# Up stage of a hybrid attention block: the last transposes of hT in four runs of four, one per step of the weights' stream

## The chip, the cores and the metric

The kernel runs on one core of one Trainium2 chip. The metric is device time in microseconds; of several runs the median is compared. The core has a matrix engine (TensorE, PE in the profile; its weight loads are PEld), a vector engine (VectorE, DVE), a scalar engine (ScalarE, ACT), GpSimd (POOL) and a sync engine (SyncE, SP) that issues most of the DMAs. Each engine works through its own instructions in order and waits for the others by semaphores.

## The reference

One layer of a decoder with 256 tokens and width 2048, in float32. The parts before the place of the change (attention of three kinds, gates, the output projection) end in a residual x. Then comes the feed-forward part:

```python
h2 = rms_norm(x, g_ffn[l])
u = causal_depthwise_conv(h2 @ w_up[l], conv_w[l], conv_b[l])   # width 2 * 5632
u_gate, u_val = jnp.split(u, 2, axis=-1)
x = x + (jax.nn.silu(u_gate) * u_val) @ w_down[l]
```

`rms_norm` divides each row by the root of its mean square and multiplies by a gain per column. The convolution is over three tokens, per channel.

## The kernel before

**Precision.** Each float32 product is made of parts: a weight piece `raw` is loaded, `hi` is its rounded copy (ScalarE, `piece`, L143), `lo` is `raw - hi` (VectorE, L144). Activations are split likewise. `wp` holds four buffers each of `raw`, `hi` and `lo`, so a cast to `hi` waits until TensorE has read the piece four back, and a load waits until the `lo` of the piece four back is made.

**The output projection** (`blocked`, name "o") adds to the residual `xres` in two halves of 1024 columns. Behind each half, two generators `hidden_T(n)` are queued (L1188), one for each 512 columns, n = 0 to 3.

**hT.** `hidden_T(n)` transposes the columns of `xres` to `hT`, the moving operand of the up stage. `transposed` makes two k tiles (one pair): four 128x128 transposes on TensorE into one PSUM bank (L197), two scaled copies on ScalarE (L183) and two subtractions on VectorE (L186). Pairs are named by their first k tile: n = 0 and 1 make pairs 0 to 6 during the second half of the output projection, n = 2 makes 8 and 10, n = 3 makes 12 and 14; 12 lies in the large tile, 14 in a tile of its own (`hT_rest`). `square_part` then takes the squares' sums of the 512 columns (L622, ScalarE). After n = 3 the root of the mean is made (`row_rstd`: L629, L607 to L612, with two activation table loads on ScalarE), written to DRAM by POOL (`rstd_row`, L1160, 256 single floats) and read back as a row for all partitions (`rbc`, L1161). The norm's row factor is thus applied only after the up product.

**The up stage** (L1274 on) goes through 11 groups of 512 channels, each with a gate half (s = 0) and a value half (s = 1). Each half is 8 steps; a step loads two k tiles of `w_up` (a piece, written u_s_k here: half s, first k tile k; the tile names in the rows below end in a buffer number), and TensorE makes 16 matmuls of it: for two k tiles and four channel tiles a `hi` matmul (L1289, 512 columns) and a `lo` matmul (L1290, 256 columns). After each step `tick()` lets up to two queued generators go one stretch on, to their next `yield`; a generator that yields a number sits out so many ticks. Step k is the one that uses k tiles k and k + 1, so hT's pair k is needed in step k of the first group.

**After the products**, `first_convs` and `second_convs` handle the first group: copies from PSUM (L1225, L1226), then `taken`: multiply by `rbc` (L1235, VectorE), the taps (L1240 to L1242), SiLU, and the split of the product. The first use of `rbc` is in the value half of the first group.

**What sets the order.** Program order by the generators' ticks, refined by a scheduler that places instructions on each engine's list; instructions given to `in_order` or `pin` keep their place. Two loads of the down stage's `kept` sums (T4, tile `raw_t_d` in the rows) share the buffers of the squares' waste output (`junk`), so they wait on SP's list for the squares.

Of the kernel before, what the change touches and what calls it, by code (L numbers as in the profile page):

```python
# [43 lines left out]
def hybrid_block(  # L44
# [38 lines left out]
    def bank(name):  # L83
        return pp.tile([P, 512], F32, tag="bank", name=name)
# [46 lines left out]
    def pin(ins):  # L131

        if pinned[0]:
            tc.keep_in_program_order(ins)
# [45 lines left out]
    def split_scaled(dsts, srcs, gs):  # L180

        for dst, src, g in zip(dsts, srcs, gs):
            pin(nc.scalar.activation(dst[:, :S], src, AF.Copy, scale=g))  # L183
        for dst, src, g in zip(dsts, srcs, gs):
            pin(
                nc.vector.scalar_tensor_tensor(  # L186
                    dst[:, S:], src, g, dst[:, :S].bitcast(F32), ALU.mult, ALU.subtract
                )
            )

    def transposed(dst, src, g, k, name, n=2):

        ps = bank(f"{name}_{k}")
        for j in range(n):
            for t in range(NT):
                pin(
                    nc.tensor.transpose(  # L197
                        ps[:, j * S + t * P : j * S + (t + 1) * P], src[:, t, (k + j) * P : (k + j + 1) * P], ident
                    )
                )  # L200
        js = range(n)
        split_scaled([dst(k + j) for j in js], [ps[:, j * S : (j + 1) * S] for j in js], [g(k + j) for j in js])
# [414 lines left out]
    def square_part(ss, src, n, name, ts=range(NT)):  # L617

        for t in ts:
            sq = junk(f"junk_{name}_{t}_{n}")  # L620
            tc.keep_in_program_order(
                nc.scalar.activation(  # L622
                    sq, src[:, t, n * 512 : (n + 1) * 512], AF.Square, accum_out=ss[:, t, n : n + 1]
                )
            )

    def row_rstd(dst, ss, name):
        tot = sm.tile([P, NT], F32, tag="tot", name=f"tot_{name}")
        nc.vector.tensor_reduce(tot, ss, AX.X, ALU.add)  # L629
        rsqrt_mean(dst, tot, NT, D, name)  # L630
# [517 lines left out]
    rbc = cst.tile([P, S], F32, tag="rbc", name="rbc")  # L1148

    def hidden_T(n):  # L1150
        yield
        transposed(hT, xres, gffn, 4 * n, "hT")
        transposed(hT, xres, gffn, 4 * n + 2, "hT")
        square_part(ssf, xres, n, "f")
        yield
        if n == 3:

            row_rstd(rstd_f, ssf, "f")
            row = dram.tile([NT, P], F32, tag="rstd_row", name="rstd_row")
            nc.gpsimd.dma_start(row.rearrange("t p -> p t"), rstd_f)  # L1160
            nc.gpsimd.dma_start(rbc, row.rearrange("t p -> (t p)").partition_broadcast(P))  # L1161
# [17 lines left out]
    for nb, plan in enumerate(o_plans):  # L1179
        X = blocked(  # L1180
            "o", w_out, nb, nb * PIECE, plan, lambda p, j: mT[p][:, j], lambda p, f: ms[p][:, f], raw_o, t4_o[nb],
            lambda n0, Y: gather(n0, Y, block),
        )
        for n in range(2):
            for t in range(NT):
                o = xres[:, t, nb * PIECE + n * 512 : nb * PIECE + (n + 1) * 512]
                nc.vector.tensor_tensor(o, o, X[t][n], ALU.add)
            later(hidden_T(2 * nb + n))  # L1188
# [211 lines left out]
```

## Time and profile before

| | |
|---|---|
| median of 3 runs | 1460.6 us (1460.43 to 1470.62) |
| profiled execution, its own time | 1459.85 us |
| its span, first to last instruction | 1458.1 us |
| instructions | 20568 |
| bytes moved by DMA | 387.64 MB, mean 266 GB/s |
| up stage on TensorE | from 741.6 us |
| granted TensorE clock | 1.00 |

All times within the execution count from the start of the span. A row of the timeline gives start, duration, engine, line, operation and operands, how many instructions are merged, and in brackets how long the engine sat idle before it and what ended that. Ends of matmuls are modelled, so pace is read from start to start. "DMA to landing" is the time from the issue of a transfer until its last byte is reported. Durations in the prediction are from this one execution.

### The profile page before, as it was taken

Reading aid. Unit: us, or ns where it says so; the run is one execution under the profiler, and the core shown is the slowest. Engines: PE = TensorE matmul, PEld = TensorE weight load, DVE = VectorE, ACT = ScalarE, POOL = GpSimd, SP = SyncE. Lnnn points to the kernel's source line nnn. Section 1 sums busy time; section 2 is a strip of 40 time slices with the busy share of each in tenths; the row PEclk is TensorE's granted clock in tenths of the full one; section 3 lists DMA queues with packets and bytes.
Section 4 is the critical chain, followed back from the end, with each engine's and each line's share of the span. In section 5 each row is a group of like instructions: output and inputs, shape, how many; then the busy total and the mean of one; then the engine's idle time right before and its main releaser. Section 6 shows DMA issues by size and latency. Waiting matters only on the chain.

```text
span 1458.1 us, 20568 instructions
## 1 busy us (share of the span) xinstructions
PE 1452.6 (100%) x7295; PEld 1228.6 (84%) x7295; DVE 1222.1 (84%) x1804; ACT 852.3 (58%) x1210; POOL 21.4 (1%) x52
## 2 busy tenths in 40 slices
PE   9999999999999999999999999999999999999998
PEld 7888888888888888888888888888888888888887
DVE  5788778776898899998987888888888877999878
ACT  6755445464564556546766656556556565676665
POOL 0000010010000000000000000000000000000000
PEclk9999999999999999999999999999999999999999
DMA  8797999777668576788877888888888866789896
GB/s 294 227 351 246 324 330 329 261 256 218 205 210 267 174 227 200 269 269 263 300 214 233 290 273 299 283 269 300 287 278 299 271 197 201 255 282 339 297 333 218
DMA packets 166502, 387.64 MB, mean 266 GB/s; under 512 B 12554, under 2 KB 29854, under 8 KB 162174
## 3 DMA queue, kind: packets, MB, share of 16 engines
q1 hardware_dynamic: 164702, 383.29, 79.7%
q10 hardware_dynamic: 1328, 2.11, 0.4%
q8 instruction: 57, 0.93, 0.3%
q0 software_dynamic: 368, 0.93, 0.2%
q14 instruction: 47, 0.39, 0.1%
HBM read 347.47 MB, written 38.80 MB: 265 GB/s over the span
## 4 chain that ended last, share of the span: by engine, by line
PE 94%; DVE 3%; issue 2%; DMA 1%; POOL 0%; ACT 0%; DVEq 0%; POOLq 0%; ACTq 0%
PE u L1289 22%; PE u L1290 11%; PE xd L362 4%; PE xd L360 4%; PE xd L361 3%; PE xg L362 3%; PE xg L360 3%; PE xg L361 3%; PE s L362 2%; PE f L362 2%; PE s L360 2%; PE f L360 2%; PE f L361 2%; PE b L362 2%; PE s L361 2%; PE b L360 2%
## 5 line engine op out<-in xcount | busy, mean ns | idle before, releaser
L1289 PE MATMUL u<-hT,hi_u 128*128 128x512 f32 x1232 | 428.3, 394 | 0.0
L1290 PE MATMUL u<-hT,lo_u 128*128 128x256 f32 x1232 | 341.3, 277 | 0.0
L144 DVE TENSOR_TENSOR lo_u<-raw_u,hi_u 128x1024 fp32r<-128x1024 f32 x176 | 215.0, 1222 | 73.3 <-ACT hi_u L143 72.5
L1289 PEld LDWEIGHTS u<-hT,hi_u 128*128 128x128 f32 x1232 | 231.0, 188 | 53.6
L143 ACT CAST hi_u<-raw_u 128x1024 fp32r<-128x1024 f32 x176 | 184.7, 1050 | 133.8 <-PE u L1289 99.4
L1290 PEld LDWEIGHTS u<-hT,lo_u 128*128 128x128 f32 x1232 | 231.3, 188 | 0.0
L355 DVE TENSOR_TENSOR lo_d<-raw_d,hi_d 128x1024 fp32r<-128x1024 f32 x88 | 106.8, 1222 | 16.5 <-ACT hi_d L354 14.1
L354 ACT CAST hi_d<-raw_d 128x1024 fp32r<-128x1024 f32 x88 | 91.8, 1054 | 39.3 <-PE xd L361 13.1
L354 ACT CAST hi_g<-raw_g 128x1024 fp32r<-128x1024 f32 (+1 forms) x80 | 77.1, 972 | 49.4 <-PE xg L361 19.4
L355 DVE TENSOR_TENSOR lo_g<-raw_g,hi_g 128x1024 fp32r<-128x1024 f32 (+1 forms) x80 | 88.6, 1119 | 4.1 <-ACT hi_g L354 4.1
L361 PE MATMUL xg<-hi_g,xT 128*128 128x512 f32 x175 | 68.1, 389 | 0.0
L362 PE MATMUL xg<-lo_g,xT 128*128 128x512 f32 x175 | 68.1, 389 | 0.0
L360 PE MATMUL xg<-hi_g,xT 128*128 128x512 f32 x175 | 68.1, 389 | 0.0
L143 ACT CAST hi_f<-raw_f 128x1024 fp32r<-128x1024 f32 (+1 forms) x40 | 38.5, 967 | 46.3 <-PE f L361 29.4
L144 DVE TENSOR_TENSOR lo_s<-raw_s,hi_s 128x1024 fp32r<-128x1024 f32 (+1 forms) x40 | 44.5, 1119 | 23.8 <-ACT hi_s L143 23.8
L1289 PE MATMUL u<-hT_rest,hi_u 128*128 128x512 f32 x176 | 62.0, 394 | 0.0
L143 ACT CAST hi_b<-raw_b 128x1024 fp32r<-128x1024 f32 x32 | 33.7, 1053 | 45.9 <-PE b L361 20.3
L143 ACT CAST hi_s<-raw_s 128x1024 fp32r<-128x1024 f32 (+1 forms) x40 | 38.4, 962 | 37.7 <-PE s L361 26.8
L1240 ACT ACTIVATE y<-u,taps 128x256 f32<-128x256 f32 x88 | 49.6, 596 | 16.8 <-DVE u L1235 16.7
L144 DVE TENSOR_TENSOR lo_f<-raw_f,hi_f 128x1024 fp32r<-128x1024 f32 (+1 forms) x40 | 44.4, 1116 | 17.4 <-ACT hi_f L143 17.2
L362 PE MATMUL xd<-lo_d,aT 128*128 128x512 f32 x148 | 57.6, 389 | 0.0
L360 PE MATMUL xd<-hi_d,aT 128*128 128x512 f32 x148 | 57.6, 389 | 0.0
(551 smaller groups left out, 3482.0 us busy)
## 6 DMA issues: line engine op xcount, KB each, us to landing
raw_u<-in_w_up_dram SPq DMA_DIRECT2D x176, 512.0 KB, 4.8
raw_g<-in_w_in_dram SPq DMA_DIRECT2D x96, 512.0 KB, 4.5
raw_d<-in_w_down_dram SPq DMA_DIRECT2D x63, 512.0 KB, 5.5
pre_d<-in_w_down_dram SPq DMA_DIRECT2D x17, 1024.0 KB, 7.4
kept_d<-pre_d SPq DMA_DIRECT2D x17, 1024.0 KB, 7.0
raw_f<-in_w_in_dram SPq DMA_DIRECT2D x32, 512.0 KB, 5.6
raw_s<-in_w_in_dram SPq DMA_DIRECT2D x32, 512.0 KB, 6.1
raw_t_d<-kept_d SPq DMA_DIRECT2D x25, 512.0 KB, 5.8
```

Of the source, the lines that this page charges most:

```text
L143: pin(nc.scalar.copy(hi[:, :m], raw[:, :m]))
L144: pin(nc.vector.tensor_tensor(lo[:, :m], raw[:, :m], hi[:, :m].bitcast(F32), ALU.subtract))
L354: nc.scalar.copy(hi[:, :n], src)
L355: nc.vector.tensor_tensor(lo[:, :n], src, hi[:, :n].bitcast(F32), ALU.subtract)
L360: fix(nc.tensor.matmul(o, lhsT=ah, rhs=w[0], start=first, stop=False))
L361: fix(nc.tensor.matmul(o, lhsT=al, rhs=w[0], start=False, stop=False))
L362: fix(nc.tensor.matmul(o, lhsT=ah, rhs=w[1], start=False, stop=last))
L1240: nc.scalar.activation(y, u[:, 2:], AF.Identity, scale=tap(2), bias=tap(3))
L1289: nc.tensor.matmul(ps[i], lhsT=hi[:, j, c], rhs=hT(k + j), start=first, stop=False)
L1290: nc.tensor.matmul(ps[i][:, :S], lhsT=lo[:, j, c], rhs=hT(k + j)[:, :S], start=False, stop=last)
```

## The change

`hidden_T` gets two more stops. n = 3 sits out two more ticks before it begins, and n = 2 and n = 3 stop between their two pairs. n = 0 and n = 1 are as before.

```diff
     def hidden_T(n):
-        yield
+        yield 2 if n == 3 else 0
         transposed(hT, xres, gffn, 4 * n, "hT")
+        if n > 1:
+            yield
         transposed(hT, xres, gffn, 4 * n + 2, "hT")
         square_part(ssf, xres, n, "f")
         yield
```

On TensorE the four pairs 8, 10, 12 and 14 stood behind each other after step 2 of the first group (sixteen transposes in a row); now pair 8 stands after step 2, pair 10 after step 4, 12 after step 6 and 14 after step 8. Lines behind the place move down by two (L1235 becomes L1237, L1289 becomes L1291).

ScalarE's list at this place, before; `hi_u` are weight casts, `hT` and `hT_rest` the copies of the pairs, `junk_f_n` the squares of column block n, L608 and L609 the root:

```order
L143 CAST hi_u_0_10_6931<-raw_u_0_10_6930 128x1024
L183 ACTIVATE hT<-hT_6805,gmix_c 128x256 x2
L183 ACTIVATE hT<-hT_6814,gmix_c 128x256 x2
L622 ACTIVATE junk_f_2_6823,ssf<-xres_again 128x512
L622 ACTIVATE junk_f_2_6825,ssf<-xres_again 128x512
L183 ACTIVATE hT<-hT_6827,gmix_c 128x256 x2
L183 ACTIVATE hT_rest<-hT_6836,gmix_c 128x256 x2
L622 ACTIVATE junk_f_3_6846,ssf<-xres_again 128x512
L622 ACTIVATE junk_f_3_6848,ssf<-xres_again 128x512
L143 CAST hi_u_0_12_6953<-raw_u_0_12_6952 128x1024
L608 ACT_TABLE_LOAD
```

And of the change, from the cast of u_0_14 on (ahead of it stand the cast of u_0_12 and the copies of pair 10 with the squares of block 2):

```order
L143 CAST hi_u_0_14_6975<-raw_u_0_14_6974 128x1024
L183 ACTIVATE hT<-hT_6871,gmix_c 128x256 x2
L143 CAST hi_u_1_0_7001<-raw_u_1_0_7000 128x1024
L183 ACTIVATE hT_rest<-hT_6902,gmix_c 128x256 x2
L622 ACTIVATE junk_f_3_6912,ssf<-xres_again 128x512
L622 ACTIVATE junk_f_3_6914,ssf<-xres_again 128x512
L143 CAST hi_u_1_2_7033<-raw_u_1_2_7032 128x1024
L608 ACT_TABLE_LOAD
L608 ACTIVATE nwt_f<-nwa_f 128x2
L609 ACT_TABLE_LOAD
L609 ACTIVATE nwy_f<-nwt_f 128x2
L143 CAST hi_u_1_4_7061<-raw_u_1_4_7060 128x1024
```

The squares of block 3 and the root stood around the cast of u_0_12; now they stand around that of u_1_2, three casts later, and no cast lies between the two table loads.

VectorE's list where the root ends, before, with the sum of the squares (L629) and the factor that POOL writes out (L612):

```order
L629 TENSOR_REDUCE tot_f<-ssf 128x2
L1219 MEMSET u_7022 128x2
L1219 MEMSET u_7024 128x2
L607 TENSOR_SCALAR nwa_f<-tot_f 128x2
L144 TENSOR_TENSOR lo_u_0_12_6954<-raw_u_0_12_6952,hi_u_0_12_6953 128x1024
L144 TENSOR_TENSOR lo_u_0_14_6976<-raw_u_0_14_6974,hi_u_0_14_6975 128x1024
L610 TENSOR_TENSOR nwt_f<-nwy_f 128x2
L611 SCALAR_TENSOR_TENSOR nwt_f<-nwt_f,nwa_f 128x2
L612 SCALAR_TENSOR_TENSOR scales<-nwt_f,nwy_f 128x2
```

And of the change:

```order
L144 TENSOR_TENSOR lo_u_1_0_7002<-raw_u_1_0_7000,hi_u_1_0_7001 128x1024
L186 SCALAR_TENSOR_TENSOR hT_rest<-hT_6902,gmix_c,hT_rest 128x256 x2
L629 TENSOR_REDUCE tot_f<-ssf 128x2
L607 TENSOR_SCALAR nwa_f<-tot_f 128x2
L144 TENSOR_TENSOR lo_u_1_2_7034<-raw_u_1_2_7032,hi_u_1_2_7033 128x1024
L610 TENSOR_TENSOR nwt_f<-nwy_f 128x2
L611 SCALAR_TENSOR_TENSOR nwt_f<-nwt_f,nwa_f 128x2
L612 SCALAR_TENSOR_TENSOR scales<-nwt_f,nwy_f 128x2
```

The factor is made behind the lo part of u_1_2 instead of u_0_14, two pieces later. The first reader of rbc (L1237) stands where it stood, between the lo parts of u_1_12 and u_1_14.

SP's list, before; `raw_t_d` are the two loads that share the squares' buffers:

```order
L142 DMA raw_u_1_2_7032<-in_w_up_dram 128x2x512
L453 DMA raw_t_d_0_11976<-kept_d_0_2252 128x512
L453 DMA raw_t_d_1_12067<-kept_d_1_2414 128x512
L142 DMA raw_u_1_4_7060<-in_w_up_dram 128x2x512
L142 DMA raw_u_1_6_7082<-in_w_up_dram 128x2x512
L142 DMA raw_u_1_8_7104<-in_w_up_dram 128x2x512
```

And of the change:

```order
L142 DMA raw_u_1_4_7060<-in_w_up_dram 128x2x512
L142 DMA raw_u_1_6_7082<-in_w_up_dram 128x2x512
L142 DMA raw_u_1_8_7104<-in_w_up_dram 128x2x512
L453 DMA raw_t_d_0_11976<-kept_d_0_2252 128x512
L453 DMA raw_t_d_1_12067<-kept_d_1_2414 128x512
L142 DMA raw_u_1_10_7126<-in_w_up_dram 128x2x512
```

The two loads moved past three loads of weights.

## The prediction

> **What bounds the kernel now.** I read the page's totals first, then the chain that ended last, then the up stage by windows.
>
> ```profile
> PE 1452.6 (100%) x7295; PEld 1228.6 (84%) x7295; DVE 1222.1 (84%) x1804; ACT 852.3 (58%) x1210; POOL 21.4 (1%) x52
> PE 94%; DVE 3%; issue 2%; DMA 1%; POOL 0%; ACT 0%; DVEq 0%; POOLq 0%; ACTq 0%
> 741.60:763.80 22.20, 22.20 (x135) 19.59 (x134) 17.24 (x30) 16.21 (x28) 0.74 (x1) 1.00 0.79 199
> 786.00:808.00 22.00, 22.00 (x129) 19.25 (x128) 22.00 (x41) 14.57 (x25) 0.00 (x0) 1.00 0.82 273
> ```
>
> The columns of the last two rows are stretch, length, then busy time of PE, PEld, DVE, ACT and POOL, granted clock, DMA share and GB/s. TensorE is busy for the whole of both stretches at a granted clock of 1.00, so nothing it waits for can be shortened here. It can gain only by doing less, and it loses as soon as an operand is late. From 786 to 808 us VectorE has not a moment free either (22.00 of 22.00), and this matters below.
>
> So the question has two halves: what do the four runs cost on TensorE itself, and does any operand come late because other engines' work moved with them?
>
> **The transposes themselves.** Here are TensorE's rows around the one run of sixteen, and a run of four elsewhere that the kernel makes already (between two matmuls of the merge).
>
> ```profile
> 747.12 0.28 PE L1290 MATMUL u<-hT,lo_u 128*128 128x256 f32 x1
> 747.24 1.91 PE L197 MATMUL hT<-ident,xres_again 128*128 128x128 f32 x16
> 748.91 0.47 PE L1289 MATMUL u<-hT,hi_u 128*128 128x512 f32 x1
> 749.22 0.27 PE L1290 MATMUL u<-hT,lo_u 128*128 128x256 f32 x1
> ...
> 473.25 0.39 PE L362 MATMUL b<-lo_b,oT 128*128 128x512 f32 x1
> 473.48 0.60 PE L1040 MATMUL mt<-ident,g 128*128 128x128 f32 x4
> 473.84 0.48 PE L360 MATMUL b<-hi_b,oT 128*128 128x512 f32 x1
> 474.15 0.40 PE L361 MATMUL b<-hi_b,oT 128*128 128x512 f32 x1
> ```
>
> From start to start, sixteen take 748.91 - 747.24 = 1.67 us, and the matmul behind them holds its place for 0.31 us (749.22 - 748.91) instead of 0.23 (473.48 - 473.25): 1.75 us in all. Four take 473.84 - 473.48 = 0.36 us, and the matmul behind them again 0.31 instead of 0.23: 0.44 us. Four such runs are 1.76 us. The change on TensorE is **+0.01 us**. I bound it by nothing gained (0) and by one further such switch of 0.08 us per added run (+0.24).
>
> Does TensorE still get hT in time? A step (two k tiles) lasts 785.04 to 787.82, that is 2.78 us (rows below). Each of the four pairs now has two whole steps between its run and its own use (14 is transposed after step 8 and used in step 14), at least 5.6 us. In that time it waits for one weight cast on ScalarE (1.05 us) and one lo part on VectorE (1.2), and is copied out at 0.7 us per pair on each (751.65 to 752.36), some 3 us together. Hidden, with over 2 us to spare; if that cover were gone, TensorE would stall by what is missing.
>
> **What moves behind them.** The squares of column block 3 (L622) are issued only after pair 14, so they now come after step 8 instead of after step 2, and the whole chain to rbc hangs on them: sum, reciprocal root, two small transfers by POOL.
>
> ```profile
> 747.32 1.05 ACT L143 CAST hi_u<-raw_u 128x1024 fp32r<-128x1024 f32 x1 [1.78 <-PE u L1289]
> 751.65 0.86 ACT L183 ACTIVATE hT_rest<-hT,gmix_c 128x256 fp32r<-128x256 f32 x2
> 752.36 0.67 ACT L622 ACTIVATE junk_f<-xres_again 128x512 f32<-128x512 f32 x1
> 753.59 1.09 ACT L143 CAST hi_u<-raw_u 128x1024 fp32r<-128x1024 f32 x1
> 754.70 1.28 ACT L608 ACT_TABLE_LOAD   x1
> 756.10 1.03 ACT L143 CAST hi_u<-raw_u 128x1024 fp32r<-128x1024 f32 x1
> 757.15 1.28 ACT L609 ACT_TABLE_LOAD   x1
> 758.45 0.20 ACT L609 ACTIVATE nwy_f<-nwt_f 128x2 f32<-128x2 f32 x1
> 759.07 0.16 DVE L612 SCALAR_TENSOR_TENSOR scales<-nwt_f,nwy_f 128x2 f32<-128x2 f32 x1
> 759.53 0.74 POOL L1160 DMA_DIRECT2D rstd_row<-scales  x1 [422.74 <-DVE scales L612]
> 768.56 0.55 POOL L1161 DMA_DIRECT2D rbc<-rstd_row  x1 [8.29 <-DMA rstd_row<-scales]
> ```
>
> Step by step, in the times of this execution. A weight cast waits until TensorE has read the piece four back, and starts 0.08 us after that step's end (747.32 against 747.24). Step 8 now ends at 747.24 + 3 x (0.44 + 2.78) = 756.9; step 10 at 760.1. The cast of u_1_0 runs 757.0 to 758.0, the two copies of pair 14 to 758.7, the two squares (753.59 - 752.36 = 1.23) to 759.9. The cast of u_1_2 must wait for step 10: 760.2 to 761.2. From a cast's end to the end of the exponential it takes 758.65 - 754.68 = 3.97 us with one other cast (1.05) between the two table loads; that cast is no longer there, so 2.92: 764.1. POOL starts 759.53 - 758.65 = 0.88 later, **at 765.0 instead of 759.53**, 5.5 us late.
>
> ```profile
> DMA to landing us min/median/max: 7.6/7.6/7.6
> ...
> 777.49 1.23 DVE L144 TENSOR_TENSOR lo_u<-raw_u,hi_u 128x1024 fp32r<-128x1024 f32 x1 [1.57 <-ACT hi_u L143]
> 778.63 0.42 DVE L1235 TENSOR_TENSOR u<-y,rbc 128x256 f32<-128x256 f32 x1
> 780.66 1.23 DVE L144 TENSOR_TENSOR lo_u<-raw_u,hi_u 128x1024 fp32r<-128x1024 f32 x1
> 783.83 1.23 DVE L144 TENSOR_TENSOR lo_u<-raw_u,hi_u 128x1024 fp32r<-128x1024 f32 x1
> 805.79 1.22 DVE L144 TENSOR_TENSOR lo_u<-raw_u,hi_u 128x1024 fp32r<-128x1024 f32 x1
> ...
> 785.04 0.39 PE L1289 MATMUL u<-hT_rest,hi_u 128*128 128x512 f32 x1
> 787.82 0.39 PE L1289 MATMUL u<-hT,hi_u 128*128 128x512 f32 x1
> 788.05 0.27 PE L1290 MATMUL u<-hT,lo_u 128*128 128x256 f32 x1
> ```
>
> The first row is the landing of rbc. Before the change rbc is there at 768.56 + 7.6 = 776.2, and its first reader, L1235, starts at 778.63, right behind the weight piece ahead of it: 2.4 us of cover. From POOL's start to the landing it takes 16.6 us, so after the change rbc is there at 765.0 + 16.6 = 781.6, and L1235 starts 3.0 us late. It stands in VectorE's order ahead of the lo parts of the weights; these are late with it. The tightest is the one that began at 783.83: done at 785.06, read by TensorE at 788.05, 2.99 us ahead. Next come 805.79 (done 807.01, needed eight steps after 788.05, at 810.2: 3.2) and 780.66 (done 781.89, needed 0.23 after 785.04: 3.4), the former because VectorE has nothing free from 786 to 808 with which to catch up. A delay of 3.0 us uses up 2.99. The stall on TensorE is **0.0 to 0.1 us**.
>
> The price of that cover gone: each further us by which rbc lands later is about a us on TensorE, once, since TensorE's own stall then restores the distance for all later pieces. The landing is the uncertain term. The nearest other rows are the two pairs of the same kind at 182 us.
>
> ```profile
> L897 POOL DMA_DIRECT2D ck_row<-logits x2: 731/796/860, 182.7 to 183.6; - x2
> DMA to landing us min/median/max: 3.0/6.1/9.0
> L899 POOL DMA_DIRECT2D ck<-ck_row x2: 554/562/569, 186.0 to 189.1; - x2
> DMA to landing us min/median/max: 6.9/7.9/9.0
> ```
>
> With 0.3 us between write and read, the shortest pair would be 3.0 + 0.3 + 6.9 = 10.2 us (rbc at 775.2, no wait at all), and the longest 9.0 + 0.3 + 9.0 = 18.3 us (783.3, 1.8 us of stall). I take 16.6, the same two transfers.
>
> The trace speaks for the long one: while the small write is under way the weights crawl.
>
> ```profile
> 762.00:770.00 8.00, 8.00 (x47) 6.98 (x47) 4.31 (x7) 3.34 (x6) 0.55 (x1) 1.00 0.70 45
> 772.35 1.05 ACT L143 CAST hi_u<-raw_u 128x1024 fp32r<-128x1024 f32 x1 [5.28 <-DMA raw_u<-in_w_up_dram]
> ```
>
> From 762 to 770 us all queues moved 45 GB/s against 273 in the window at 786, and a cast waited 5.28 us for its piece. That slump moves along, to about 767.5 to 775.5. It then catches u_1_12 and later pieces; u_1_12 would land at 777.8 as its forerunner did 2.35 us after the slump, its lo part would be done at 780.1, and TensorE wants it two steps before 788.05, at 782.5: hidden, with 2.4 us over. The two loads of d's T4 on SP's queue move behind u_1_8, since they wait for the same squares; they are read only in the down stage, some 450 us on, and cost nothing.
>
> **The sum.** 0.01 for the runs and 0.05 for the stall on a profiled execution of 1459.85 us (span 1458.1), which lies 0.75 below the median of 1460.6. On the median's scale: 1460.7 us. One per cent, 14.6 us, is about what a measurement of this kernel can tell from no change.
>
> **The rivals.** *The cover holds.* If the small write is quicker where it now lies, as the shortest pair at 182 us was, rbc lands before 778.6 and L1235 doesn't wait. Time 1460.6. Against it stands the slump; I give 0.27. The Trainium skill ("DMA: Bandwidth & Descriptors", section on the anatomy of one DMA on the gpsimd path) puts such a transfer at about 2.0 us plus its bytes over 436 GB/s; by it the pair of 1 KB and 128 KB would take some 4.6 us, an estimate, and this rival would be certain. The trace disagrees: 9.0 us until the write is done, 16.6 for both.
>
> *Slower: the landing is later than 781.6.* The place is L1235 on VectorE at the second half of the first group; it decides from 781.6 on, at a us per us, up to 1.8 us by the longest pair; a slump longer by the same amount could take another us from the pieces at 777 to 783. Times of 1461.5 to 1463.5, still within 1%. For it: other loads queue up around the write than before. 0.20. To reach 14.6 us this mechanism would need rbc at 796, for which no row speaks: 0.02.
>
> *It gives time back, or doesn't act.* The order on the engines shows four separate runs, so it acts. A gain on TensorE needs idle time there, and the up stage has none: 0.01 for over 1% faster.
>
> **Chances and range.** The forecast (stall 0 to 1 us, 1460.4 to 1461.6) has 0.50, the covered case 0.27, the later landing 0.20, the rest 0.03. The range runs from 1459.6, the covered case less 1.0 (the profiled execution lay 0.75 below the median without any change), to 1463.3, the long bound with 0.9 us of further slump. Within 1%: 0.97.
>
> **What would show it.** Four runs of four L197 on PE, each 0.36 us; POOL's L1160 near 765 us; L1237 (L1235 before) on VectorE starting near 781.7 with a wait on the DMA of rbc; TensorE's stretch from 741 to 808 with under 1 us idle. I am wrong if TensorE waits for an hT pair, if rbc lands after 785, or if a lo part is late somewhere past 810 us.

## The result, and the profile after

The change costs time. Its median over 22 runs is **1469.26 us** (1460.53 to 1471.42), beside 1460.49 us (1459.59 to 1470.62) for the kernel before, also over 22 runs. The ratio on record is 1.0039, with a 95% interval of 1.0024 to 1.0053 (the quotient of the two medians is 1.0060): within 1%, as forecast, but above the forecast's range (1459.6 to 1463.3).

The median can't be understood without one fact: the executions of this program have two lengths with little in between, at a granted clock of 1.00 in both. Of the change, 15 of 22 took 1469.0 to 1471.4 us and 7 took 1460.5 to 1462.2; of before, 2 of 22 took 1469 or more, and 20 took 1459.6 to 1462.9. I call them long and short executions. The change turns a rare long execution into the usual one.

The first profile of the change caught a short execution (1460.73 us). The change was therefore profiled again, as the first experiment below, and that profile is of a long one (1470.26 us). First the page's totals of the short one:

```profile
PE 1452.4 (100%) x7295; PEld 1228.7 (84%) x7295; DVE 1222.3 (84%) x1804; ACT 851.4 (58%) x1210; POOL 21.4 (1%) x52
```

The same row of the long one:

```profile
PE 1461.6 (100%) x7295; PEld 1233.1 (84%) x7295; DVE 1223.2 (83%) x1804; ACT 852.3 (58%) x1210; POOL 21.4 (1%) x52
```

TensorE makes the same 7295 instructions and is busy all the time in both, 9.2 us longer in the long one. So little of the loss is waiting. The groups of the up stage's matmuls show where it went (columns: count, then busy time and mean ns of one, then idle time before). Before:

```profile
L1289 PE MATMUL u<-hT,hi_u 128*128 128x512 f32 x1232 | 428.3, 394 | 0.0
L1290 PE MATMUL u<-hT,lo_u 128*128 128x256 f32 x1232 | 341.3, 277 | 0.0
```

The long execution of the change:

```profile
L1291 PE MATMUL u<-hT,hi_u 128*128 128x512 f32 x1232 | 436.8, 399 | 0.0
L1292 PE MATMUL u<-hT,lo_u 128*128 128x256 f32 x1232 | 346.1, 281 | 0.1
```

The same matmuls are a little longer each. Since ends of matmuls are modelled, I read the pace from counts: the view of windows, over 300 us in the middle of the up stage, over 90 us behind the last run of transposes. Before:

```profile
850.00:1150.00 300.00, 300.00 (x1733) 262.35 (x1732) 256.43 (x418) 177.36 (x274) 0.00 (x0) 1.00 0.86 286
```

The short execution of the change:

```profile
850.00:1150.00 300.00, 300.00 (x1733) 262.43 (x1732) 256.46 (x420) 177.34 (x273) 0.00 (x0) 1.00 0.86 287
```

The long execution of the change, in which the second row is the stretch of the forecast's stall:

```profile
850.00:1150.00 300.00, 300.00 (x1700) 260.30 (x1699) 251.52 (x406) 172.72 (x263) 0.00 (x0) 1.00 0.83 279
786.00:808.00 22.00, 21.52 (x120) 18.28 (x120) 21.24 (x39) 17.44 (x29) 0.00 (x0) 1.00 0.75 238
```

In 300 us TensorE makes 1733 matmuls in one kind of execution and 1700 in the other, busy throughout (300.00) at a clock of 1.00. From start to start, where the cut ends of the window don't count, a pair of one hi and one lo matmul takes 0.3467 us in before and in the short execution, and 0.3533 in the long one. Single matmuls follow each other at two fixed patterns: the quick one repeats after two pairs (231, 113, 232, 118 ns), the slow one after three (233, 117, 241, 120, 236, 113 ns). I call them the quick and the slow **rhythm**.

The sum of it: of the stage's 1408 pairs, some 25 are slow in before (ahead of its run) or quick in the long execution (between two of its runs); for the other 1383, 6.7 ns each make 9.2 us. TensorE's waits at 786 to 790 us, shown below, cost 1.0 us more. That is 10.2, and from its first matmul to its last the up stage takes 489.84 us before and 500.05 in the long execution: 10.2 more, of the 10.4 us between the two profiled executions (1459.85 and 1470.26).

Where does the rhythm change? Before enters the up stage slow. The run of sixteen at 747.24 (its rows stand in the prediction) leaves it quick: the matmul behind the run is followed by its lo after 0.31 us, and that by the next hi after 0.11. It stays so to the end of the stage. Here are two of the four runs of the change, the third and the fourth, by TensorE's timeline of the short execution:

```profile
753.96 0.60 PE L197 MATMUL hT<-ident,xres_again 128*128 128x128 f32 x4
754.32 0.47 PE L1291 MATMUL u<-hT,hi_u 128*128 128x512 f32 x1
754.63 0.27 PE L1292 MATMUL u<-hT,lo_u 128*128 128x256 f32 x1
754.74 0.40 PE L1291 MATMUL u<-hT,hi_u 128*128 128x512 f32 x1
...
757.17 0.60 PE L197 MATMUL hT<-ident,xres_again 128*128 128x128 f32 x4
757.53 0.48 PE L1291 MATMUL u<-hT,hi_u 128*128 128x512 f32 x1
757.85 0.28 PE L1292 MATMUL u<-hT,lo_u 128*128 128x256 f32 x1
757.96 0.40 PE L1291 MATMUL u<-hT,hi_u 128*128 128x512 f32 x1
```

The difference is in hundredths: 0.31 and 0.11 behind the third run (313 and 113 ns), 0.32 and 0.11 behind the fourth (318 and 117). The third leaves TensorE quick, as before's run of sixteen did. The first, second and fourth leave it slow, in both executions alike. So behind the last run both stream slowly; what made one of them short came later.

It came at the place of the forecast's stall. POOL's and VectorE's timeline, short execution:

```profile
765.49 0.74 POOL L1162 DMA_DIRECT2D rstd_row<-scales  x1 [427.70 <-DVE scales L612]
775.17 0.55 POOL L1163 DMA_DIRECT2D rbc<-rstd_row  x1 [8.95 <-DMA rstd_row<-scales]
...
782.28 0.43 DVE L1237 TENSOR_TENSOR u<-y,rbc 128x256 f32<-128x256 f32 x1 [0.30 <-DMA rbc<-rstd_row]
787.48 1.23 DVE L144 TENSOR_TENSOR lo_u<-raw_u,hi_u 128x1024 fp32r<-128x1024 f32 x1
```

Long execution, with TensorE's rows:

```profile
775.65 0.55 POOL L1163 DMA_DIRECT2D rbc<-rstd_row  x1 [9.50 <-DMA rstd_row<-scales]
783.27 0.42 DVE L1237 TENSOR_TENSOR u<-y,rbc 128x256 f32<-128x256 f32 x1 [0.94 <-DMA rbc<-rstd_row]
...
785.80 0.40 PE L1291 MATMUL u<-hT_rest,hi_u 128*128 128x512 f32 x1
786.59 0.39 PE L1292 MATMUL u<-hT_rest,lo_u 128*128 128x256 f32 x1 [0.39 <-DVE lo_u L144]
786.81 0.39 PE L1291 MATMUL u<-hT_rest,hi_u 128*128 128x512 f32 x1
...
789.28 0.40 PE L1291 MATMUL u<-hT,hi_u 128*128 128x512 f32 x1
789.76 0.39 PE L1292 MATMUL u<-hT,lo_u 128*128 128x256 f32 x1
789.98 0.39 PE L1291 MATMUL u<-hT,hi_u 128*128 128x512 f32 x1
```

rbc was read 0.99 us later in the long one, and there TensorE waited for lo parts, twice: the lo at 786.59 came 0.79 us behind its hi (785.80) instead of 0.23, the one at 789.76 came 0.48 behind instead of 0.24, and the next matmul took 0.1 more to follow each time (786.81 and 789.98). In all 1.0 us. In the short one nothing waited, but it was close. Here are TensorE's weight loads at the piece whose lo part was finished at 788.71 (787.48 + 1.23):

```profile
788.24 0.19 PEld L1291 LDWEIGHTS u<-hT_rest,hi_u 128*128 128x128 f32 x1
788.36 0.19 PEld L1292 LDWEIGHTS u<-hT_rest,lo_u 128*128 128x128 f32 x1
788.60 0.19 PEld L1291 LDWEIGHTS u<-hT,hi_u 128*128 128x128 f32 x1
788.76 0.19 PEld L1292 LDWEIGHTS u<-hT,lo_u 128*128 128x128 f32 x1
```

A lo's weights are otherwise loaded 0.12 us behind the hi's; this time 0.16: it began 0.05 us behind the end of the lo part, as the two loads that waited in the long execution did (786.59 behind 786.53, 789.76 behind 789.71). The matmul itself wasn't late. From 758 to 788 us the pairs took 0.3533 us; from this place on they took 0.3467, and so the execution was short. That this load made the difference is not shown, only that the pace changes there. In the long one the two real waits left the stream slow, 0.3533 to the end of the stage.

### The profile page after: what moved, and what is told of

It is laid out like the page before. It is cut to its first block, busy times and chain, and to the rows that moved or that the text cites. A ratio compares the mean times of both kernels' runs of the same rounds, so it can differ in the third digit from the quotient of the medians.

```text
span 1459.0 us, 20569 instructions
## 1 busy us (share of the span) xinstructions
PE 1452.4 (100%) x7295; PEld 1228.7 (84%) x7295; DVE 1222.3 (84%) x1804; ACT 851.4 (58%) x1210; POOL 21.4 (1%) x52
## 4 chain that ended last, share of the span: by engine, by line
PE 97%; DMA 1%; issue 1%; DVE 0%; SPq 0%; POOL 0%; ACT 0%; POOLq 0%; DVEq 0%
PE u L1291 22%; PE u L1292 11%; PE xg L361 4%; PE xg L360 4%; PE xg L362 4%; PE xd L361 4%; PE xd L362 3%; PE xd L360 3%; PE s L362 2%; PE f L362 2%; PE f L360 2%; PE s L360 2%; PE f L361 2%; PE b L360 2%; PE s L361 2%; PE b L362 2%
## 5 line engine op out<-in xcount | busy, mean ns | idle before, releaser
L1291 PE MATMUL u<-hT,hi_u 128*128 128x512 f32 x1232 | 429.3, 394 | 0.0
L1291 PEld LDWEIGHTS u<-hT,hi_u 128*128 128x128 f32 x1232 | 231.1, 188 | 53.6
L1291 PE MATMUL u<-hT_rest,hi_u 128*128 128x512 f32 x176 | 62.1, 394 | 0.0
```

The lines of the kernel that those rows point to most:

```text
L1291: nc.tensor.matmul(ps[i], lhsT=hi[:, j, c], rhs=hT(k + j), start=first, stop=False)
```

## The experiments

The expectations name their theories by letters. A: the long executions come from rbc's delay, through the lo parts. B: the separate runs disturb TensorE itself, through a slower pace behind them. C: a weight transfer is held up by POOL's small write at its new place. D, which makes B precise: there are two rhythms, and what interrupts the stream decides which one follows. E, formed later as D's rival: each further run of four costs time by itself. All times are medians with their range; each ratio is against runs of the kernel before on the same chip (1460.68, 1459.90 and 1460.08 us in three sets).

### The change again, and its parts one by one

The change, word for word:

> The changed kernel once more, to see an execution of the longer kind (most of its executions took 1469 to 1471 us, some 1461 to 1462, and the profile at hand is one of the short ones). Theory A (rbc comes late, the lo parts behind its first reader on VectorE come late, TensorE waits): two executions in three near 1469.5; in a profile of such a one TensorE has lost some 8 to 9 us, and the loss begins at a matmul that waits for a lo part between 777 and 812 us. Rival B (the four separate runs of transposes disturb TensorE itself): the loss lies between 747 and 758 us, or in a slower pace of matmuls behind it, with no late lo part. Rival C (a transfer is held up by the small write at its new place): the loss begins where a cast waits for a raw piece longer than 6 us.

1470.01 us (1460.02 to 1471.45, 10 runs: 7 long, 3 short), ratio 1.0048 (1.0028 to 1.0067). Its profile is the long one shown above.

**Four runs, but the root as early as before.** Squares of block 2 and 3 and the root keep their places in the steps; pairs 12 and 14 are transposed behind them.

```diff
-        transposed(hT, xres, gffn, 4 * n, "hT")
-        transposed(hT, xres, gffn, 4 * n + 2, "hT")
+        if n < 3:
+            transposed(hT, xres, gffn, 4 * n, "hT")
+            if n < 2:
+                transposed(hT, xres, gffn, 4 * n + 2, "hT")
         square_part(ssf, xres, n, "f")
         yield
+        if n == 2:
+            transposed(hT, xres, gffn, 4 * n + 2, "hT")
...
+            yield
+            transposed(hT, xres, gffn, 4 * n, "hT")
+            yield
+            transposed(hT, xres, gffn, 4 * n + 2, "hT")
```

> Four runs of four as in the change, but the squares of block 3 and the root stay where they were before the change (squares behind step 2, root behind step 4); pair 12 and 14 follow behind steps 6 and 8. Theory A: rbc is read no later than before the change, all executions as before it, 1460 to 1462 us, hardly any at 1469. Rival B: like the change, most executions at 1469 to 1471. Rival C: like before, as the small write lies where it lay.

1470.11 us (1469.71 to 1471.29, 4 runs, all long), ratio 1.0062 (1.0047 to 1.0077). POOL's timeline, a weight load and the window of this kernel (L1298 is lo here):

```profile
758.73 0.74 POOL L1164 DMA_DIRECT2D rstd_row<-scales  x1 [420.68 <-DVE scales L612]
...
775.16 0.19 PEld L1298 LDWEIGHTS u<-hT,lo_u 128*128 128x128 f32 x1 [0.28 <-DVE lo_u L144]
...
850.00:1150.00 300.00, 300.00 (x1700) 260.21 (x1700) 251.61 (x404) 172.37 (x262) 0.00 (x0) 1.00 0.84 279
```

The write starts 0.8 us earlier than before the change, rbc's first reader doesn't wait for it, and the stream is slow all the same. One lo part is late in this profile: its cast had waited 6.25 us for a weight piece, a sign like the one that C names, and the matmul at 775.16 came 0.35 us behind its hi instead of 0.24. That cost 0.22 us with the matmul behind it. The pairs take 0.3533 us from the last run on, ahead of this wait and behind it, so it didn't make the stream slow. A falls in so far as it needs a late rbc; that no wait at all is needed is shown by the next kernel.

**The change without POOL's transfers.** VectorE fills rbc; the norm's row factor is left out.

```diff
-            nc.gpsimd.dma_start(row.rearrange("t p -> p t"), rstd_f)
-            nc.gpsimd.dma_start(rbc, row.rearrange("t p -> (t p)").partition_broadcast(P))
+            nc.vector.tensor_copy(rbc[:, 0:NT], rstd_f)
+            nc.vector.memset(rbc[:, NT:], 1.0)
```

> The change without POOL's two transfers: rbc is filled by VectorE with ones (two columns with the factors), so the output lacks the row factor of the last norm. Nothing waits for rbc any more, and there is no small write to DRAM in the up stage. Theory A and rival C: all executions at 1459 to 1462 us. Rival B: most executions still at 1469 to 1471 us.

1469.82 us (1468.44 to 1470.74, 4 runs, all long), ratio 1.0058 (1.0043 to 1.0073). The window of this kernel:

```profile
850.00:1150.00 300.00, 300.00 (x1700) 260.02 (x1700) 251.60 (x404) 172.39 (x262) 0.00 (x0) 1.00 0.84 279
```

No matmul of the up stage waits, neither transfer is there, and yet TensorE makes 1700 matmuls in the same 300 us. Neither the transfers nor a late lo part are needed for a long execution: A and C both fall as what the long executions need, and the slow pace of B is left.

**One run of sixteen as before, but the root late.** The sum of squares takes in nothing (0 times a column) of the cast of u_1_0, so it waits for that.

```diff
+    newest = [None]
...
-        yield
+        yield 6 if n == 3 else 0
         if n == 3:
+            seen = newest[0][:, 0, 0:1].bitcast(F32)
+            nc.vector.scalar_tensor_tensor(ssf[:, 0, 0:1], seen, 0.0, ssf[:, 0, 0:1], ALU.mult, ALU.add)
...
+                newest[0] = hi
```

> One run of sixteen as before the change, but the root is made to wait for the cast of u_1_0 (zero times a column of it is added to a sum), so that POOL's write starts near 767 us instead of 759.5. Theory A: the longer kind of execution in most runs though the transposes are as before, 1469 to 1471 us. Rival B: as before the change, 1460 to 1462 us. Rival C: like the change, 1469 to 1471.

1466.21 us (1459.91 to 1471.24, 10 runs: 5 long, 5 short), ratio 1.0024 (1.0000 to 1.0049). The profile is of a long one. TensorE's timeline, in which L1293 is hi and L1294 lo:

```profile
785.64 0.39 PE L1293 MATMUL u<-hT_rest,hi_u 128*128 128x512 f32 x1
786.37 0.39 PE L1294 MATMUL u<-hT_rest,lo_u 128*128 128x256 f32 x1 [0.33 <-DVE lo_u L144]
...
789.05 0.40 PE L1293 MATMUL u<-hT,hi_u 128*128 128x512 f32 x1
789.54 0.39 PE L1294 MATMUL u<-hT,lo_u 128*128 128x256 f32 x1
```

From the run of sixteen up to here the stream was quick (0.3467); after the two waits it is slow (0.3533). So a wait can turn it this way too: the waits cost about 1 us, and the 1279 pairs behind them 8.5 (the stage takes 499.36 us, 9.5 more than before's). The late rbc is neither needed for the loss nor harmless: with the transposes of before, five of ten executions are long here, against 4 of 70 of the kernel before.

### Length and place of the runs

**Two runs of eight**, behind steps 2 and 6: the change without its stop between the pairs, and `yield 2 if n == 3 else 0` kept.

```diff
     def hidden_T(n):
-        yield
+        yield 2 if n == 3 else 0
```

> The sixteen transposes in two runs of eight, behind steps 2 and 6. Theory D (the matmul stream of the up stage has two stable rhythms, 0.346 and 0.353 us per hi/lo pair; every run of transposes draws anew which one follows, and it then lasts for the stage unless TensorE is made to wait): whichever rhythm follows the second run at 757 us lasts, so the time is 1460 to 1462 us with pairs at 0.346, or 1469 to 1471 us with pairs at 0.353, and the last run alone decides. Rival E (the more separate runs, the longer; the loss adds up per run): between the two, near 1463 us.

1460.14 us (1459.63 to 1461.77, 9 runs, all short), ratio 1.0003 (0.9993 to 1.0013). E had put it near 1463 us. Both runs leave the stream quick. The second, by the timeline:

```profile
753.21 1.04 PE L197 MATMUL hT<-ident,xres_again 128*128 128x128 f32 x8
754.00 0.47 PE L1289 MATMUL u<-hT,hi_u 128*128 128x512 f32 x1
754.32 0.27 PE L1290 MATMUL u<-hT,lo_u 128*128 128x256 f32 x1
754.43 0.40 PE L1289 MATMUL u<-hT,hi_u 128*128 128x512 f32 x1
```

**The one run of sixteen, a step later** (behind step 4):

```diff
     def hidden_T(n):
-        yield
+        yield 1 if n > 1 else 0
```

> One run of sixteen as before the change, but one step later (behind step 4). Theory D with the run of sixteen leaving the quick rhythm: 1460 to 1462 us, pairs at 0.346 us from the run on. If the place of the run rather than its length sets what follows: 1469 to 1471 us possible. Rival E: 1460 to 1462.

1469.54 us (1468.72 to 1470.12, 3 runs, all long), ratio 1.0065 (1.0045 to 1.0085).

```profile
750.42 1.91 PE L197 MATMUL hT<-ident,xres_again 128*128 128x128 f32 x16
752.09 0.48 PE L1289 MATMUL u<-hT,hi_u 128*128 128x512 f32 x1
752.40 0.28 PE L1290 MATMUL u<-hT,lo_u 128*128 128x256 f32 x1
752.52 0.40 PE L1289 MATMUL u<-hT,hi_u 128*128 128x512 f32 x1
```

The stream leaves this run slow, and no matmul waits. (The root moves a little too in these two kernels: POOL's write starts at 761.91 and 762.70 instead of 759.53. No lo part is late in either profile.) This is the strongest pair of the study: two runs instead of one cost nothing, and the same one run a step later costs all of it. So it isn't the number of runs, nor their length alone. The run of sixteen entered the slow pattern at one place of its three pairs before (the gaps ahead of it 241, 120, 236, 120 ns) and at another here (232, 118, 241, 121).

**The change with sixteen more transposes** behind step 10 (of a weight piece, into a bank that nobody reads), to set the rhythm back:

```diff
+                if (f0, s, k) == (0, 0, 10):
+                    extra = bank("extra")
+                    seen = hi[:, 1, 384:512].bitcast(F32)
+                    for i in range(16):
+                        nc.tensor.transpose(extra[:, (i % 4) * P : (i % 4 + 1) * P], seen, ident)
```

> The change with sixteen transposes more in one run behind step 10 (of a weight piece, into a bank that nobody reads; 1.75 us of work). Theory D: the stream falls into the quick rhythm at 762 us and stays there, 1462 to 1464 us in most executions, 7 us less than the change though it does more. Rival E: 1471 to 1473 us.

1470.35 us (1462.08 to 1472.29, 7 runs: 4 long, 3 short), ratio 1.0052 (1.0029 to 1.0076). I had expected the run to leave the stream quick. In the profiled execution it left it slow (315 and 117 ns). A long run is no reliable cure.

**The kernel before with four more transposes**, in the fifth group, behind step 8 of its gate half: the same lines, with `(f0, s, k) == (16, 0, 8)` and `range(4)`.

> The kernel before the change with four transposes more in the middle of the up stage (group 5 of 11, gate half, behind step 8, near 937 us; 0.44 us of work). Theory D: what follows may be either rhythm; if a run of four leaves the slow one as the last run of the change did, pairs go from 0.346 to 0.353 us there and the time is 1460.5 + 0.4 + about 850 pairs x 0.0071 = 1467 us. If the quick rhythm survives: 1461 us. Rival E: 1461 us.

1466.76 us (1465.28 to 1467.41, 4 runs), ratio 1.0045 (1.0029 to 1.0061). By the timeline, then the window:

```profile
936.06 0.60 PE L1298 MATMUL extra<-ident,hi_u 128*128 128x128 f32 x4
936.41 0.48 PE L1289 MATMUL u<-hT,hi_u 128*128 128x512 f32 x1
936.73 0.28 PE L1290 MATMUL u<-hT,lo_u 128*128 128x256 f32 x1
936.84 0.40 PE L1289 MATMUL u<-hT,hi_u 128*128 128x512 f32 x1
...
850.00:1150.00 300.00, 300.00 (x1711) 261.40 (x1710) 252.54 (x408) 174.44 (x266) 0.00 (x0) 1.00 0.82 281
```

This is the disputed cost by itself. Four transposes, 0.44 us with the switch, far from hT, the root and rbc, make the stage 6.15 us longer than before's (495.99 against 489.84). Pairs take 0.3467 us ahead of them and 0.3533 behind, up to the stage's end at 1238.8: (1238.8 - 936.4) / 0.3533 = 856 pairs, times 6.7 ns, are 5.7 us, and with the run 6.15. The sum closes for the stage. (The profiled execution is 7.34 us longer than before's; its up stage also began 1.25 us later, at 742.84.)

### Is it the alternation, and does each run cost?

**Hi and lo in groups of four.** For each k tile, four hi matmuls and then four lo ones, with the transposes of before and with those of the change.

```diff
+                    cs = [slice(i * P, (i + 1) * P) for i in range(4)]
                     for i in range(4):
-                        c = slice(i * P, (i + 1) * P)
-                        nc.tensor.matmul(ps[i], lhsT=hi[:, j, c], rhs=hT(k + j), start=first, stop=False)
-                        nc.tensor.matmul(
...
+                        in_order(nc.tensor.matmul(ps[i], lhsT=hi[:, j, cs[i]], rhs=hT(k + j), start=first, stop=False))
+                    for i in range(4):
+                        in_order(nc.tensor.matmul(
...
```

> The kernel before the change with the up stage's matmuls in another order: per k tile the four hi matmuls, then the four lo matmuls, instead of hi and lo in turn. If the two rhythms belong to the alternation of 512 and 256 columns (theory D), they are gone: one pace, the same in every execution. From the trace, matmuls of 512 columns follow each other at 0.227 us in the output projection and 128-column transposes at 0.109, so a pair would take 0.336 us, 0.010 less than now, and the time is 1460.5 - 1408 x 0.010 = 1446 us (estimate). If lo matmuls behind each other take as long as now: 1460 us.

> The change with the same other order of the matmuls. Theory D: the same time as the kernel grouped so without the change, within 1 us, as the four runs cost 0.01 us more and there is no second rhythm to fall into (1446 us, estimate). If the runs of four do harm by themselves: 9 us more than that.

1466.81 us (1466.13 to 1467.19) and 1466.99 us (1466.34 to 1467.54), 4 runs each; ratios 1.0044 (1.0026 to 1.0062) and 1.0047 (1.0031 to 1.0062). The window of the first:

```profile
850.00:1150.00 300.00, 300.00 (x1712) 262.16 (x1711) 251.99 (x408) 172.19 (x266) 0.00 (x0) 1.00 0.81 283
```

Both kernels have 1712 matmuls in this window: one pace, 0.3508 us per pair from start to start, between the two rhythms. The hoped-for 1446 us was wrong, since a lo behind a lo still takes 0.118 us and a hi behind a hi 0.233. But with this order the change costs 0.2 us, less than either range is wide. Its price of 9 us belongs to the alternating stream.

**A fifth run of four** in the change without transfers, so that nothing waits: the lines of the sixteen, with `range(4)`.

> The change without POOL's two transfers (rbc filled by VectorE, so the output lacks the row factor of the last norm) and with a fifth run of four transposes behind step 10 (of a weight piece, into a bank that nobody reads; 0.44 us). Without the fifth run all four executions were of the long kind, 1468 to 1471 us. Theory D: the fifth run draws anew: either quick pairs (0.346 us) from 761 us on and 1461 us, or slow ones (0.353) and 1470 us, and since no wait on rbc follows, all executions alike. Rival E (loss per run): 1471 to 1473 us.

1460.95 us (1460.08 to 1470.22, 9 runs: 6 short, 3 long), ratio 1.0019 (0.9993 to 1.0044). The profile is of a short one:

```profile
761.01 0.60 PE L1300 MATMUL extra<-ident,hi_u 128*128 128x128 f32 x4
761.36 0.47 PE L1291 MATMUL u<-hT,hi_u 128*128 128x512 f32 x1
761.68 0.27 PE L1292 MATMUL u<-hT,lo_u 128*128 128x256 f32 x1
761.79 0.40 PE L1291 MATMUL u<-hT,hi_u 128*128 128x512 f32 x1
```

E falls: with one run of four more, six of nine executions are short, against none of four without it, and the median is 8.9 us lower (1460.95 against 1469.82). I had expected all executions to be alike. They aren't. No matmul waits in the profile of a short one, and a long one wasn't profiled; that the same instructions can come out of a run either way is the likely reading, not a shown one.

## Why the prediction was wrong

**The step that failed** is the first term: "The change on TensorE is +0.01 us", bounded by 0 and +0.24. The 0.01 itself is right: each run of four takes 0.36 us and the matmul behind it 0.31 to 0.32, as in the rows used for it. What was wrong is that a run's cost ends with the matmul behind it. The choice of rhythm acts on every pair until something interrupts the stream again, here 1383 pairs at 6.7 ns. The last run of the change leaves the stream slow where before's only run had left it quick: 9.2 us, in about two executions of three. The bound priced one further switch per run; no bound and no rival priced the stream behind it.

The profile of before held the warning. Ahead of the run of sixteen twelve pairs take 4.24 us (742.65 to 746.89), 0.3533 each, and behind it a pair takes 0.3467; I read single gaps around the run and took the pace for a constant.

**The stall through rbc: right in mechanism and place, mis-sized in the landing.** Forecast: POOL's write at 765.0, rbc's reader at 781.7, 0.0 to 0.1 us of stall. Found, in the short and in the long execution: the write at 765.49 and 765.41, the reader at 782.28 and 783.27, and a stall of none in the one execution and 1.0 us in the other. The write took longer than the 8.29 us taken over from before (a wait of 8.95 and 9.50), so the case "later landing" is the one that came. Its arithmetic held: the reader is 3.65 and 4.64 us later than before's 778.63, TensorE itself some 0.8 later (its slow rhythm, and a stage that began 0.1 to 0.2 later), so of the lead of 2.99 some 0.1 should be left in the one and 0.9 be missing in the other. Counted as a stall it is a tenth of the loss. (The longest pair, with rbc at 783.3, gives 1.7 us by the prediction's own sum, not 1.8.) But its second effect, that it can turn the rhythm, wasn't foreseen: of the kernels whose last run left the profiled stream slow, those with the root as late as in the change have 13 short executions in 39 (the change in two sets, and with sixteen more transposes), those with the root earlier or without the transfers have none in 11 (root early, run a step later, no transfers). This fits the weight load at 788.76, but I have only one profile of a short one, and the runs are few.

**"The cover holds"** (0.27) is out: L1237 waited in both profiles. The Trainium skill ("DMA: Bandwidth & Descriptors", section on the anatomy of one DMA) gives a formula by which a 1 KB transfer takes about 2.0 us, an estimate; the waits of 8.95 and 9.50 us behind the write again disagree with it.

**hT in time, T4, the moved slump**: right. No matmul waited for hT. The slump moved: from 767.5 to 775.5 us of the short execution the queues carried 31 GB/s, TensorE was busy for 8.00 of the 8.00 us, and no matmul came late through it.

**Slower by over 1%** was 0.02 and didn't happen: even the long executions are 0.6% above before. The prediction took 1% for about the least that can be told from no change; the intervals here tell 0.4% from none.

**What stays open.** The runs show that a run of transposes, or a wait, can change the rhythm, and how much that costs. The long and short executions that weren't profiled are put to the rhythms by their times alone. The runs don't show what inside TensorE makes two rhythms, nor a rule by which one could tell the outcome of an entry. One regularity of the profiles is no more than that: wherever a run of four was entered from a quick stream (the fourth run of the change, the run in the fifth group), it was left slow. Its place among the runs doesn't decide what a run leaves: the third run left the stream quick in both profiles of the change and slow (314 ns) with the root early. Nor do they show why 4 of 70 executions of the kernel before were long.

## What to carry to other kernels

Where one engine is busy all the time, measure the pace of its stream (instructions per 100 us, or start to start) ahead of and behind each interruption before pricing an insertion by its own duration; two paces in one trace at one clock are a warning that a small edit may choose between them. A repeated profile and some ten runs belong to such a kernel, since one execution may show either pace. In this kernel two runs of eight were free and four runs of four were not; the run of sixteen moved by a step shows that such an outcome doesn't carry over to another place unmeasured.

## What the runs showed of the hardware

- An alternating stream of hi (512 columns) and lo (256) matmuls has two lasting rhythms at a granted clock of 1.00: 0.3467 and 0.3533 us per pair, 1.9% apart, each kept up for over 400 us. Four hi and four lo in turn have one pace, 0.3508.
- In one profile a weight load that came 0.04 us late, without a visible delay of its matmul, was followed by the other rhythm for the rest of the stage. The Trainium skill ("TensorE: Matmul & The Clock Gate", section on the back-to-back issue gap) says that the spacing in a stream of weight loads and matmuls is set by both, pipelined; this row fits that. It gives one spacing for a size; these traces show two for the same pair.
- In one profile of a quick stream, two waits that cost about 1 us (785.64 to 789.54 us with the root late) were followed by a slow stream that cost 8.5: what follows a wait can cost many times its length.
